# Two small operations a search step, sample digits by block transpose, and a limit for GpSimd on weight rests in a two-layer decoder step

## The chip, the cores and the metric

The kernel runs on one core of one Trainium2 chip. The metric is the device time of one execution in microseconds; the time of a kernel is the median of several runs.

Names of engines in this document: PE is TensorE, DVE is VectorE, ACT is ScalarE, POOL is GpSimd, SP is the engine whose queue starts most transfers.

## The reference, cut to what matters

One inference step of a decoder with two layers, for a prompt of 1024 tokens and 8 sample sequences with 1024 cached tokens each. Layer 0 is forgetting attention beside a gated recurrence, layer 1 is sparse attention, and a feed-forward block follows each. The change lies in layer 1, in the choice of keys:

```python
def dsa_attend(qpos, q, qi, wi, k, v, ki, topk):
    dots = jnp.einsum('bqhd,bkd->bqhk', qi, ki).astype(jnp.float32)
    score = jnp.einsum('bqhk,bqh->bqk', jax.nn.relu(dots), wi.astype(jnp.float32))
    causal = kpos[None, None, :] <= qpos[None, :, None]
    _, idx = lax.top_k(jnp.where(causal, score, -jnp.inf), topk)   # topk = 256
    ...   # attention of q over the chosen keys only
```

Each query has 1024 (prompt, causal) or 1025 (sample) scores and keeps the 256 largest. Everything is float32.

## The kernel before, in words

**How the program is put in order.** Work is written as Python generators ("streams"). Each yields the cost in nanoseconds that its author assumes for what it just emitted, and a driver always resumes the stream with the smallest virtual time. So the order in which instructions are emitted, and with it, mostly, the order of each engine's queue, follows from the yielded numbers; a planner of the framework can still move instructions, and a manual order edge (`late`) ties some matmuls behind the dense products. An engine works its queue strictly in order: an instruction that waits holds up all behind it. A yielded cost is no time on the chip, but it moves where an instruction stands in the queue.

**Layer 1, the stretch that matters.** The main stream multiplies the normed activations by 17 blocks of 128 columns of the projection weights (`dense_cols`). Each block is loaded, rounded by ACT to the hi part (`whif`), the rest (`wlof`) is made by DVE, and PE does 3 products for each of 8 x 3 pieces. Beside it run three kinds of streams:

- `gen_idx` makes the indexer scores of 128 queries (a row block i) against (i + 1) * 128 keys, for i = 2..7 in the groups [2, 3], [4, 5], [6, 7], and starts `top_select` for each group. (Blocks 0 and 1 keep every key.)
- `top_select` finds for every query the 256th largest score, by a search over the 31 bits of the float from the top down: 31 steps, each of which counts how many scores are at or above a candidate. In a step of the kernel before, DVE makes the candidate (`cd = F ^ (1 << b)`); each of the two row blocks is counted, by ACT (a Sign with its sum, `tjk<-sc,small` on ACT) or by DVE (a compare with its sum, L1993); DVE makes `d` from the counts, and then the new `F`: three small DVE operations of 128 x 2 elements. `NACT` says how many of a group's two blocks ACT counts: both of group 2, one of group 4 (640 wide) and one of group 6 (896 wide). DVE counts the other, 768 and 1024 wide; for bits 30 to 16 on a bf16 copy (`top`) that POOL makes. A step yields `early` before the projection is finished and `cost` after. At the end come some whole-row operations that write the mask.
- `gen_dsa_dec` does the same for the 8 samples by hexadecimal digits: 8 steps, in each of which 16 partitions of a sample try 16 candidates. DVE counts (L2263, 1025 wide) and compares with 256; a matmul with a 128 x 128 constant (L2268) adds the comparisons of each 16 partitions, and DVE reads the sum from PSUM. Afterwards the chosen keys' positions are computed (among it the transposes and matmuls at L2324), the keys gathered, and the sample attention done.

When the 17 blocks are done, the attention of layer 1 starts: 8 row blocks by 4 key heads, row block i only once its mask is there. It has scores (`s`, L530), a DVE operation that adds the mask and finds the largest (L533), ACT exponentials, transposes, and products with V (`o`, L2099 up to row block 4 and L2103 from 5). Then come the output projection, and layer 1's feed-forward block.

**POOL** does the rotary products (`raw`, `shf`) and rests (`r1l`) of the projected blocks in this stretch, with operations of 2.4 us each.

The class `Weights` counts the weight blocks that it has split in `self.ns`. The list that it walks through has 21 + 8 blocks for layer 0, 4 for the feed-forward block's last part, 17 + 8 for layer 1, and 4 more: 62, so `ns` runs from 0 to 61, and layer 1's projection has the numbers 33 to 49. Two places ask for an interval of it:

```python
        def phase(n):
            return "" if n < 25 or 93 <= n < 110 else "f"
                    hi, lo = U(..., "whi" + ph), U(..., "wlo" + ph)
                    (gt if self.ns < 3 or 93 <= self.ns < WP else tt)(lo, raw, _r(hi), SUB)
```

`gt` is POOL's operation, `tt` DVE's; a tile's name has an "f" outside the interval.

Of the kernel before, what the change touches and what calls it, by code (L numbers as in the profile page):

```python
# [8 lines left out]
F32 = mybir.dt.float32  # L9
F32R = mybir.dt.float32r  # L10
BF = mybir.dt.bfloat16
# [9 lines left out]
S = 1024  # L21
# [11 lines left out]
def _consts():  # L33
# [31 lines left out]
    c["bm8x128"] = (b8[:, None] == p[None, :] // 16).astype(f)  # L65
    c["grp16"] = ((p[:, None] // 16 == p[None, :] // 16) & (p[:, None] % 16 >= 1)).astype(f)
    c["bd16"] = (p[:, None] // 16 == p[None, :] // 16).astype(f)
# [19 lines left out]
PTAGS.update({k: ("bl", 2) for k in ("ia", "ib", "ka", "kb", "do")})  # L87
WP, DY = 0, 2200.0
NACT = {2: 2, 4: 1, 6: 1}
QID = 0  # L90
# [4 lines left out]
SPARE = {3: (1,), 4: (1,), 5: (1, 3), 6: (1, 3), 7: (1, 3)}  # L95
BFC = True
PLAIN = range(5)
# [62 lines left out]
def build(tc, I, O, C):  # L160
    nc = tc.nc
    with ExitStack() as ctx:
# [68 lines left out]
        def gcopy(out, in_):  # L231
            return (nc.gpsimd if BFC == True else nc.vector).tensor_copy(out=out, in_=in_)

# [1670 lines left out]
        def gen_idx():  # L1904
# [11 lines left out]
            for grp in ([2, 3], [4, 5], [6, 7]):  # L1916
                if grp[0] == 2:
                    s2 = U([128, 1040], F32, "sc")
                    sc[2], sc[3] = s2[:, :384], s2[:, 384:896]
                else:  # L1920
                    for i in grp:
                        sc[i] = U([128, S], F32, "sc")[:, :(i + 1) * 128]
                for i in grp:
                    masks[i] = sc[i].bitcast(BF)[:, :(i + 1) * 128]
                if grp[0] == 2:
                    for t in range(4):
                        yield from need("l1.qi%d" % t)
                        for i in grp:
                            yield from idx_scores(i, 2 * t, 2)
                else:  # L1930
                    for i in grp:
                        yield from idx_scores(i, 0, 8)
                for i in grp:
                    w = sc[i].shape[1]
# [31 lines left out]
        def top_select(grp, rows):  # L1966
# [5 lines left out]

            na = NACT[grp[0]]
            A = slice(0, na)
            F, cd, d = [small("1", [128, 2], nm, bufs=3, dt=I32) for nm in ("tF", "tcd", "td")]
            cnt, thr = small("1", [128, 2], "tcnt", bufs=3), small("1", [128, 2], "tthr", bufs=3)
# [4 lines left out]

            top = {}
            if BFC:
                for j in range(na, 2):
                    n = rows[j][1]
                    top[j] = V([128, 1040], BF, "top")[:, :n]
                    gcopy(top[j], rows[j][0].bitcast(BF).rearrange("p (n e) -> p n e", e=2)[:, :, 1])

            def count(j, th, op, b=0):
                sj, n = rows[j][:2]  # L1990
                if b >= 16 and BFC:
                    sj = top[j]
                nc.vector.tensor_scalar(out=jk[:, 1, :n], in0=sj, scalar1=th, scalar2=None, op0=op, op1=ADD,  # L1993
                                        accum_out=cnt[:, j:j + 1])

            for j in range(2):
                nc.gpsimd.memset(thr[:, j:j + 1], 2 * TOPK - 0.5 - rows[j][1] if j < na else TOPK - 0.5)
            cost, early = CM[grp[0]] * (n1 / 0.96 + 600), CE[grp[0]] * (n1 / 0.96 + 600)
# [5 lines left out]
            ts(F, d, 31, 31, ALU.logical_shift_left, ALU.arith_shift_right)  # L2004
            if na:
                ts(F[:, A], F[:, A], -0x80000000, None, ALU.bitwise_xor)
# [29 lines left out]
            for j, (sj, n, m) in enumerate(rows):  # L2036
                th = thr[:, j:j + 1]
                eq = jk[:, 1]
                ts(eq[:, :n], sj, th, None, ALU.is_equal)
# [109 lines left out]
        def gen_dsa_dec():  # L2149
# [92 lines left out]
            dma(out=dig, in_=C["dig"])  # L2242
            grp = V([128, 128], F32, "grpc")
            dma(out=grp, in_=C["grp16"])
            ti = [small("1", [128, 1], "tdi%d" % x, dt=I32) for x in range(4)]
# [10 lines left out]
            for step in range(8):  # L2256
# [7 lines left out]
                                        op0=ALU.is_ge, op1=ADD, accum_out=cn)  # L2264
                ts(cn, cn, TOPK - 0.5, None, ALU.is_ge)
                yield DY
                p = bank()
                late(mm(p[:, 0:1], lhsT=grp, rhs=cn, start=True, stop=True))  # L2268
                yield 700.0
                sh_ = 28 - 4 * step  # L2270
                if step == 0:
                    ts(sf, p[:, 0:1], 7.5, -16.0, ALU.is_ge, MUL)
                    tt(sf, sf, p[:, 0:1], ADD)
# [358 lines left out]
```

## Time and profile before

| | us |
|---|---|
| median of 3 runs | 2834.91 |
| lowest and highest run | 2833.43, 2839.29 |
| profiled execution | 2833.61 |
| its span, first to last instruction | 2831.9 |

Outside the span lie 1.7 us. In the span PE is busy 90%, DVE 79%, ACT 47% and POOL 47% of the time. Shares over the whole span hide that the stages have different limits, so the rows below are taken from single stretches, in us from the start of the span: 1445 to 1690 (the projection of layer 1 with the searches), 1690 to 1770 and 1770 to 1880 (attention of layer 1 with the searches of groups 4 and 6), and 1880 to 2000 (attention without a search).

### The profile page before, as it was taken

To read this page: it belongs to the slowest core of one execution; us is meant where nothing else is said; L and a number is where in the kernel's file an instruction comes from. 1 tells how busy PE (TensorE), PEld (TensorE's weight loads), DVE (VectorE), ACT (ScalarE), POOL (GpSimd) and SP (SyncE) were. 2 spreads that over 40 slices of the span, in tenths; PEclk is the share of its full clock that TensorE was granted. 3 is DMA by queue.
4 is the path that set the end of the run, shared out by engine and by line. 5 is a ranking of instruction groups with operands and counts; after the bars stand their busy time and mean duration, and the time that the engine had idled before them with its cause. 6 is when DMAs were issued, how large, how long until landed. Compare 5 with 4: busy or idle time off the path is not lost.

```text
span 2831.9 us, 48456 instructions
## 1 busy us (share of the span) xinstructions
PE 2556.9 (90%) x17916; PEld 2391.4 (84%) x17916; DVE 2230.6 (79%) x4125; ACT 1328.7 (47%) x2726; POOL 1337.9 (47%) x992
## 2 busy tenths in 40 slices
PE   7988889989999899999888758999979999899998
PEld 6977788989999899999777744567979999898998
DVE  4466887787777899986468999998477887899995
ACT  4235766344434433433256457779333343533331
POOL 2376454345555666620544525133135555667630
PEclk9999999999999999999989868999989999999999
DMA  4844567304444634322353325321303444644331
GB/s 132 269 149 142 164 213 251 131 16 139 136 154 135 205 126 143 128 98 93 97 154 106 119 77 129 81 59 31 128 23 109 143 147 145 207 135 131 125 105 61
DMA packets 272095, 363.30 MB, mean 128 GB/s; under 512 B 25184, under 2 KB 200456, under 8 KB 271604
## 3 DMA queue, kind: packets, MB, share of 16 engines
q1 hardware_dynamic: 217124, 290.48, 32.1%
q0 software_dynamic: 15120, 49.81, 5.3%
q10 hardware_dynamic: 39616, 19.93, 2.5%
q8 instruction: 141, 2.31, 0.3%
q14 instruction: 94, 0.77, 0.1%
HBM read 252.19 MB, written 108.00 MB: 127 GB/s over the span
## 4 chain that ended last, share of the span: by engine, by line
PE 47%; DVE 21%; issue 4%; ACT 4%; DMA 3%; POOL 2%; SPq 0%; ACTq 0%; DVEq 0%; POOLq 0%
PE d L1501 10%; PE d L1503 9%; PE d L1502 9%; DVE fdu L218 4%; PE d L339 3%; PE d L341 3%; PE d L340 3%; PE s L530 2%; PE o L2099 2%; PE t L251 2%; DVE xT L218 1%; DVE x1a L218 1%; DVE small L229 1%; DVE fd L218 1%; DVE tjk L1993 1%
## 5 line engine op out<-in xcount | busy, mean ns | idle before, releaser
L1501 PE MATMUL d<-xoph,fs 128*128 128x258 f32 x768 | 221.6, 289 | 19.7 <-ACT z L215 13.0
L221 POOL TENSOR_TENSOR fraw<-fraw,small 128x1024 f32<-128x1024 f32 x64 | 134.4, 2104 | 209.9 <-DMA fraw<-in_ffn_w 181.7
L218 DVE TENSOR_TENSOR xT<-xT,d 128x258 f32<-128x258 f32 (+1 forms) x472 | 185.5, 424 | 44.6 <-PE d L341 26.9
L1502 PE MATMUL d<-xoph,fs 128*128 128x258 f32 x768 | 219.2, 286 | 0.0
L1503 PE MATMUL d<-xoph,fs 128*128 128x258 f32 x768 | 218.4, 285 | 0.0
L339 PE MATMUL d<-xh,whif 128*128 128x344 f32 (+1 forms) x616 | 201.9, 329 | 11.4 <-DVE small L226 5.7
L341 PE MATMUL d<-xh,wlof 128*128 128x344 f32 (+1 forms) x616 | 198.0, 325 | 3.9 <-DVE wlof L218 3.9
L340 PE MATMUL d<-xl,whif 128*128 128x344 f32 (+1 forms) x616 | 200.6, 326 | 0.0
L221 POOL TENSOR_TENSOR z<-z 128x516 f32<-128x516 f32 x112 | 168.8, 1507 | 47.0 <-DMA d_zp<-z 39.2
L215 ACT ACTIVATE s<-s,small 128x128 f32<-128x128 f32 (+7 forms) x192 | 149.7, 782 | 66.8 <-DVE small L533 65.5
L339 PE MATMUL d<-xh,whi 128*128 128x344 f32 x504 | 169.9, 338 | 11.4 <-ACT whi L215 5.9
L341 PE MATMUL d<-xh,wlo 128*128 128x344 f32 x504 | 165.0, 330 | 12.2 <-DVE wlo L218 11.8
L1501 PEld LDWEIGHTS d<-xoph,fs 128*128 128x128 f32 x768 | 147.2, 192 | 23.8 <-ACT z L215 16.3
L340 PE MATMUL d<-xl,whi 128*128 128x344 f32 x504 | 167.2, 332 | 0.0
L218 DVE TENSOR_TENSOR fdu<-fraw,fdu 128x256 fp32r<-128x256 f32 x168 | 165.0, 993 | 0.0
L1501 PE MATMUL d<-zoph,fdu 128*128 128x258 f32 x448 | 129.7, 292 | 26.9 <-DVE xT L218 13.7
L1502 PEld LDWEIGHTS d<-xoph,fs 128*128 128x128 f32 x768 | 147.6, 192 | 0.6 <-DVE xoph L218 0.6
L1503 PEld LDWEIGHTS d<-xoph,fs 128*128 128x128 f32 x768 | 147.7, 192 | 0.0
L1503 PE MATMUL d<-xop,fl 128*128 128x258 f32 x512 | 146.3, 286 | 1.4 <-DVE fl L218 1.4
L1501 PE MATMUL d<-xop,fl 128*128 128x258 f32 x512 | 146.4, 286 | 0.0
L1502 PE MATMUL d<-xop,fl 128*128 128x258 f32 x512 | 146.2, 286 | 0.0
L251 PE MATMUL t<-small,s 128*128 128x128 f32 x864 | 139.4, 280 | 5.7 <-DVE tm L218 3.4
(484 smaller groups left out, 9902.2 us busy)
## 6 DMA issues: line engine op xcount, KB each, us to landing
fraw<-in_ffn_w SPq DMA_DIRECT2D x120, 512.0 KB
zr<-d_zp SPq DMA_DIRECT2D x98, 516.0 KB
d_zp<-z POOLq DMA_DIRECT2D x56, 516.0 KB, 3.2
kp<-in_cache_fox_kv SPq DMA_DIRECT2D x64, 256.0 KB
vp<-in_cache_fox_kv SPq DMA_DIRECT2D x64, 256.0 KB
q1b<-d_q ACTq DMA_DIRECT2D x32, 512.0 KB
d_zp<-z SPq DMA_DIRECT2D x28, 516.0 KB
wraw<-in_ab_w_in SPq DMA_DIRECT2D x21, 512.0 KB
```

What stands on the lines that cost most here:

```text
L215: return nc.scalar.activation(out=out, in_=in_, func=func, **kw)
L218: return nc.vector.tensor_tensor(out=out, in0=a, in1=b, op=op)
L221: return nc.gpsimd.tensor_tensor(out=out, in0=a, in1=b, op=op)
L251: return nc.tensor.transpose(out, in_, ident[:n, :n])
L339: mm(ps, lhsT=wh, rhs=ah, start=(j == 0), stop=False)
L340: mm(ps, lhsT=wh, rhs=al, start=False, stop=False)
L341: i = mm(ps, lhsT=wl, rhs=ah, start=False, stop=(j == last))
L530: mm(p[:, :m], lhsT=lh[x], rhs=ks[:, k0:k0 + m], start=(x == 0), stop=(x == 1 and not dg))
L1501: mm(o, lhsT=wh[:, k], rhs=hi[:, cols], start=(start and k == 0), stop=False, skip_group_check=not start)
L1502: mm(o, lhsT=wh[:, k], rhs=lo[:, cols], start=False, stop=False, skip_group_check=not start)
L1503: i = mm(o, lhsT=wl[:, k], rhs=hi[:, cols], start=False, stop=(k == nk - 1), skip_group_check=not start)
L2099: mm(po[:64], lhsT=VF[g // 2][:, kb, 64 * (g % 2):64 * (g % 2) + 64], rhs=ph, start=(kb == 0), stop=(kb == i))
```

## The change

- **Search step.** `F` now carries the next candidate itself, so that a step has two small operations behind the counts instead of one ahead and two behind: `e` is (count below the bound) * 2^b, and `F = (F ^ 2^(b-1)) ^ e`. `SGP` is False, so its branch for POOL is not built.
- **Who counts.** `ONA = (2, 4)`: ACT counts both blocks of groups 2 and 4, all at the width of the wider block (512 and 768), with the narrower block's last 128 columns filled with `LOW`; DVE counts both of group 6 (896 and 1024). The bf16 copies `top` (2 POOL copies, 2 buffers of the V pool) are gone.
- **Sample digits.** The matmul L2268 of each of the 8 steps is gone. DVE writes the comparison into 32 columns, transposes 32 x 32 blocks, multiplies by a constant of 128 x 32 and sums over 32 columns. The virtual cost of 700 for the matmul goes (8 times), and two later yields grow, from 26000 to 32000 and from 4000 to 10000.
- **Weight rests.** `WP` goes from 0 to 110 in the condition above.

```diff
-WP, DY = 0, 2200.0
-NACT = {2: 2, 4: 1, 6: 1}
+WP, DY = 110, 2200.0
+ONA, SGP = (2, 4), False
...
-                    sc[2], sc[3] = s2[:, :384], s2[:, 384:896]
+                    sc[2], sc[3] = s2[:, :512], s2[:, 512:1024]
...
+                if grp[0] in ONA:
+                    nc.gpsimd.memset(sc[grp[0]][:, (grp[0] + 1) * 128:], LOW)
...
-            na = NACT[grp[0]]
+            na = 2 if grp[0] in ONA else 0
...
-                    top[j] = V([128, 1040], BF, "top")[:, :n]
-                    gcopy(top[j], rows[j][0].bitcast(BF).rearrange("p (n e) -> p n e", e=2)[:, :, 1])
...
+            ts(F, F, (1 << 30) - (0x80000000 if na else 0), None, ALU.bitwise_xor)
             yield cost
             for b in range(30, -1, -1):
-                ts(cd, F, 1 << b, None, ALU.bitwise_xor)
                 for j in range(2):
-                    if j < na:
-                        act(jk[:, 0, :rows[j][1]], rows[j][0], AF.Sign, bias=cd[:, j:j + 1].bitcast(F32),
+                    if na:
+                        act(jk[:, 0, :n1], rows[j][0], AF.Sign, bias=F[:, j:j + 1].bitcast(F32),
                             accum_out=cnt[:, j:j + 1])
                     else:
-                        count(j, cd[:, j:j + 1].bitcast(F32), ALU.is_ge, b)
-                stt(d, cnt, 1.0, thr, MUL, ALU.is_ge)
-                stt(F, d, b, F, ALU.logical_shift_left, ALU.bitwise_xor)
+                        count(j, F[:, j:j + 1].bitcast(F32), ALU.is_ge)
...
+                    ts(e, cnt, least, float(1 << b), ALU.is_lt, MUL)
+                    stt(F, e, (1 << b) >> 1, F, ALU.bitwise_xor, ALU.bitwise_xor)
                 yield cost if "l1.in" in flags else early
...
-                ts(cn, cn, TOPK - 0.5, None, ALU.is_ge)
+                ts(c32, cn.to_broadcast([128, 32]), TOPK - 0.5, None, ALU.is_ge)
+                nc.vector.transpose(t32, c32)
+                tt(t32, t32, g32, MUL)
+                nc.vector.tensor_reduce(out=cn, in_=t32, axis=AX.X, op=ADD)
                 yield DY
-                p = bank()
-                late(mm(p[:, 0:1], lhsT=grp, rhs=cn, start=True, stop=True))
-                yield 700.0
...
-                    ts(sh, p[:, 0:1], float(1 << sh_), None, MUL)
+                    ts(sh, cn, float(1 << sh_), None, MUL)
...
-            yield 26000
+            yield 32000
...
-            yield 4000
+            yield 10000
```

## Rows read from the trace of the kernel before

**Rows 1.** Busy time of each engine in four stretches: PE, PEld, DVE, ACT, POOL, PE clock.
```profile
1445.00:1690.00 245.00, 177.67 (x986) 166.85 (x986) 222.51 (x459) 140.63 (x332) 113.44 (x64) 0.84 0.37 110
1690.00:1770.00 80.00, 64.26 (x247) 35.70 (x246) 71.33 (x252) 60.30 (x164) 35.92 (x38) 0.81 0.53 132
1770.00:1880.00 110.00, 106.76 (x498) 59.70 (x497) 102.00 (x293) 79.20 (x181) 18.95 (x17) 1.00 0.28 74
1880.00:2000.00 120.00, 114.92 (x667) 92.98 (x666) 98.28 (x258) 110.84 (x231) 48.95 (x56) 1.00 0.16 47
```

**Rows 2.** Waits, 1445 to 1690: waiter, what ended it, us, times, longest.
```profile
ACT tjk L215 <- DVE small L226: 56.9, 20, 7.0
...
PEld b L2268 <- DVE small L226: 18.0, 4, 6.2
PE b L2268 <- DVE small L226: 16.7, 4, 6.0
...
PE b L2324 <- DVE small L229: 13.6, 1, 13.6
DVE small L229 <- ACT tjk L215: 11.6, 10, 2.2
```

**Rows 3.** DVE by line and shape, 1445 to 1690: busy us, mean ns | idle before.
```profile
L226 DVE TENSOR_SCALAR small<-small 128x2 int32<-128x2 int32 x65 | 25.6, 395 | 0.9
L229 DVE SCALAR_TENSOR_TENSOR small<-small 128x2 int32<-128x2 int32 x55 | 22.7, 414 | 0.5
...
L1993 DVE TENSOR_SCALAR_CACHE_REDUCE tjk<-top,small 128x768 bf16<-128x768 bf16 x15 | 15.1, 1004 | 0.1
...
L1993 DVE TENSOR_SCALAR_CACHE_REDUCE tjk<-sc,small 128x768 bf16<-128x768 f32 x4 | 4.0, 1012 | 0.1
```

**Rows 4.** DVE in order of time, near 1610: start us, us, operation.
```profile
1609.39 2.25 DVE L226 TENSOR_SCALAR small<-small 128x2 int32<-128x2 int32 x1
...
1612.76 2.28 DVE L229 SCALAR_TENSOR_TENSOR small<-small 128x2 int32<-128x2 f32 x1
```

**Rows 5.** POOL in order of time, the same moments.
```profile
1609.20 2.42 POOL L221 TENSOR_TENSOR raw<-raw,ropc 128x1032 f32<-128x1032 f32 x1 [1.35 <-DVE small L229]
1611.58 3.44 POOL L221 TENSOR_TENSOR shf<-shf,rops 128x1032 f32<-128x1032 f32 x1
```

**Rows 6.** The search's tile over the span: durations min/median/max, first and last start.
```profile
L1993 DVE TENSOR_SCALAR_CACHE_REDUCE tjk<-top,small x30: 995/1132/1279, 1503.6 to 1769.1; 128x768 bf16<-128x768 bf16 x15, 128x1024 bf16<-128x1024 bf16 x15
```

**Rows 7.** DVE by line and shape, 1650 to 1670.
```profile
L2333 DVE TENSOR_REDUCE tmpd<-tmpd 128x16 f32<-128x128 f32 x1 | 0.4, 363 | 0.0
...
L226 DVE TENSOR_SCALAR small<-small 128x2 f32<-128x2 f32 x2 | 0.3, 158 | 0.0
```

**Rows 8.** DVE by line and shape, 1690 to 1770.
```profile
L1993 DVE TENSOR_SCALAR_CACHE_REDUCE tjk<-sc,small 128x768 bf16<-128x768 f32 x14 | 14.1, 1010 | 0.2
...
L226 DVE TENSOR_SCALAR small<-small 128x2 int32<-128x2 int32 x23 | 3.8, 179 | 0.3
```

**Rows 9.** DVE by line and shape, 1770 to 1880.
```profile
L226 DVE TENSOR_SCALAR small<-small 128x2 int32<-128x2 int32 x19 | 3.5, 186 | 0.3
...
L1993 DVE TENSOR_SCALAR_CACHE_REDUCE tjk<-sc,small 128x896 bf16<-128x896 f32 x2 | 2.3, 1144 | 0.0
```

**Rows 10.** ACT by line and shape, 1770 to 1880.
```profile
L215 ACT ACTIVATE tjk<-sc,small 128x896 bf16<-128x896 f32 x16 | 16.6, 1035 | 5.6 <-DVE small L226 5.5
...
L215 ACT ACTIVATE s<-s,small 128x768 f32<-128x768 f32 x7 | 6.5, 934 | 6.2 <-DVE small L533 6.1
L215 ACT ACTIVATION_READ_ACCUMULATOR tjk<-sc,small 128x1 f32 x16 | 3.1, 191 | 0.0
```

**Rows 11.** ACT by line and shape, 1445 to 1690.
```profile
L215 ACT ACTIVATE tjk<-sc,small 128x640 bf16<-128x640 f32 x19 | 15.7, 828 | 30.6 <-DVE small L226 23.7 <-DVE small L229 6.8
...
L215 ACT ACTIVATE tjk<-sc,small 128x896 bf16<-128x896 f32 x6 | 6.2, 1040 | 0.2
```

**Rows 12.** The tile wlof, 1300 to 1700: durations min/median/max, first and last start.
```profile
L218 DVE TENSOR_TENSOR wlof<-wrawf,whif x16: 1211/1226/2506, 1322.9 to 1663.9; 128x1024 fp32r<-128x1024 f32 x16
```

More of the change, by code (lines that the diff above doesn't have):

```diff
@@ L65, in _consts @@
     c["bm8x128"] = (b8[:, None] == p[None, :] // 16).astype(f)
-    c["grp16"] = ((p[:, None] // 16 == p[None, :] // 16) & (p[:, None] % 16 >= 1)).astype(f)
+    f32 = np.arange(32)
+    c["grp32"] = ((p[:, None] % 32 // 16 == f32[None, :] // 16) & (f32[None, :] % 16 >= 1)).astype(f)
     c["bd16"] = (p[:, None] // 16 == p[None, :] // 16).astype(f)
@@ L95 @@
 SPARE = {3: (1,), 4: (1,), 5: (1, 3), 6: (1, 3), 7: (1, 3)}
-BFC = True
 PLAIN = range(5)
@@ L231, in gcopy @@
         def gcopy(out, in_):
-            return (nc.gpsimd if BFC == True else nc.vector).tensor_copy(out=out, in_=in_)
+            return nc.gpsimd.tensor_copy(out=out, in_=in_)
         def bcast(src):
@@ L1918, in gen_idx @@
                     s2 = U([128, 1040], F32, "sc")
-                    sc[2], sc[3] = s2[:, :384], s2[:, 384:896]
+                    sc[2], sc[3] = s2[:, :512], s2[:, 512:1024]
                 else:
                     for i in grp:
-                        sc[i] = U([128, S], F32, "sc")[:, :(i + 1) * 128]
+                        sc[i] = U([128, S], F32, "sc")[:, :(grp[1] + 1) * 128 if grp[0] in ONA else (i + 1) * 128]
                 for i in grp:
@@ L1932, in gen_idx @@
                         yield from idx_scores(i, 0, 8)
+                if grp[0] in ONA:
+                    nc.gpsimd.memset(sc[grp[0]][:, (grp[0] + 1) * 128:], LOW)
                 for i in grp:
-                    w = sc[i].shape[1]
+                    w = (i + 1) * 128
                     nc.gpsimd.affine_select(out=sc[i][:, w - 128:w], in_=sc[i][:, w - 128:w], pattern=[[-1, 128]],
@@ L1966, in top_select @@
         def top_select(grp, rows):
-            na = NACT[grp[0]]
+            na = 2 if grp[0] in ONA else 0
             A = slice(0, na)
-            F, cd, d = [small("1", [128, 2], nm, bufs=3, dt=I32) for nm in ("tF", "tcd", "td")]
+            F, d, e = [small("1", [128, 2], nm, bufs=3, dt=I32) for nm in ("tF", "td", "tcd")]
             cnt, thr = small("1", [128, 2], "tcnt", bufs=3), small("1", [128, 2], "tthr", bufs=3)
@@ L1980, in top_select, with count @@
             nc.gpsimd.memset(cu[:, 0:1], 0.0)
[L1982 to L1985, printed above, removed]
-                    top[j] = V([128, 1040], BF, "top")[:, :n]
-                    gcopy(top[j], rows[j][0].bitcast(BF).rearrange("p (n e) -> p n e", e=2)[:, :, 1])
-            def count(j, th, op, b=0):
+            def count(j, th, op):
                 sj, n = rows[j][:2]
-                if b >= 16 and BFC:
-                    sj = top[j]
-                nc.vector.tensor_scalar(out=jk[:, 1, :n], in0=sj, scalar1=th, scalar2=None, op0=op, op1=ADD,
+                nc.vector.tensor_scalar(out=jk[:, 1, :n], in0=sj[:, :n], scalar1=th, scalar2=None, op0=op, op1=ADD,
                                         accum_out=cnt[:, j:j + 1])
-            for j in range(2):
-                nc.gpsimd.memset(thr[:, j:j + 1], 2 * TOPK - 0.5 - rows[j][1] if j < na else TOPK - 0.5)
+            least = 2 * TOPK - 0.5 - n1 if na else TOPK - 0.5
             cost, early = CM[grp[0]] * (n1 / 0.96 + 600), CE[grp[0]] * (n1 / 0.96 + 600)
@@ L2004, in top_select @@
             ts(F, d, 31, 31, ALU.logical_shift_left, ALU.arith_shift_right)
-            if na:
-                ts(F[:, A], F[:, A], -0x80000000, None, ALU.bitwise_xor)
+            ts(F, F, (1 << 30) - (0x80000000 if na else 0), None, ALU.bitwise_xor)
             yield cost
             for b in range(30, -1, -1):
-                ts(cd, F, 1 << b, None, ALU.bitwise_xor)
                 for j in range(2):
-                    if j < na:
-                        act(jk[:, 0, :rows[j][1]], rows[j][0], AF.Sign, bias=cd[:, j:j + 1].bitcast(F32),
+                    if na:
+                        act(jk[:, 0, :n1], rows[j][0], AF.Sign, bias=F[:, j:j + 1].bitcast(F32),
                             accum_out=cnt[:, j:j + 1])
                     else:
-                        count(j, cd[:, j:j + 1].bitcast(F32), ALU.is_ge, b)
-                stt(d, cnt, 1.0, thr, MUL, ALU.is_ge)
-                stt(F, d, b, F, ALU.logical_shift_left, ALU.bitwise_xor)
+                        count(j, F[:, j:j + 1].bitcast(F32), ALU.is_ge)
+                if na and SGP:
+                    nc.gpsimd.tensor_scalar(out=d, in0=F, scalar1=(1 << b) >> 1, scalar2=None, op0=ALU.bitwise_xor)
+                    nc.gpsimd.tensor_scalar(out=e, in0=cnt, scalar1=least, scalar2=float(1 << b), op0=ALU.is_lt, op1=MUL)
+                    gt(F, d, e, ALU.bitwise_xor)
+                else:
+                    ts(e, cnt, least, float(1 << b), ALU.is_lt, MUL)
+                    stt(F, e, (1 << b) >> 1, F, ALU.bitwise_xor, ALU.bitwise_xor)
                 yield cost if "l1.in" in flags else early
@@ L2038, in top_select @@
                 eq = jk[:, 1]
+                sj = sj[:, :n]
                 ts(eq[:, :n], sj, th, None, ALU.is_equal)
@@ L2242, in gen_dsa_dec @@
             dma(out=dig, in_=C["dig"])
-            grp = V([128, 128], F32, "grpc")
-            dma(out=grp, in_=C["grp16"])
+            grp = V([128, 3, 32], F32, "grpc")
+            dma(out=grp[:, 0], in_=C["grp32"])
+            g32, c32, t32 = [grp[:, x] for x in range(3)]
             ti = [small("1", [128, 1], "tdi%d" % x, dt=I32) for x in range(4)]
```

4 lines of the change are left out of this document (2 added, 2 removed).

## Prediction, written before the changed kernel was run

> **What bounds the kernel now.** I went from the page's shares to the chain of waits, saw that the searches lie in it between 1445 and 1880 us, and then took the busy time of the engines by stretch [rows 1]. Three stretches differ.
>
> In stretch A (1445 to 1690, projection and searches) DVE is busy 222.5 of 245 us, PE only 177.7, at a mean granted clock of 0.84, ACT 140.6. So DVE sets the pace there. The waits of A say the same from the other side [rows 2]: ACT waits 56.9 us for a DVE operation of 128 x 2 elements ahead of its Sign, PE waits 18.0 + 16.7 = 34.7 us for DVE's comparison ahead of the digit matmul, and 13.6 us at L2324. DVE itself waits for another engine mainly in one place: 11.6 us for ACT's Sign.
>
> In stretch B (1690 to 1770, attention begins) DVE is busy 71.3 of 80 us and PE 64.3. In stretch C (1770 to 1880) PE is busy 106.8 of 110 us at full clock and DVE 102.0: both are nearly full, and DVE has 8.0 us left. From 1880 on no search runs.
>
> What makes DVE slow in A is to be seen in the small operations. The same form takes 395 ns on average in A [rows 3] and 179 and 186 ns in B and C [rows 8, 9]. The difference is POOL: an operation of 2 elements took 2.25 us while POOL's rotary product of 2.42 us ran, and the next one 2.28 us beside a product of 3.44 us [rows 4, 5]. The counts don't suffer from it: 995 to 1279 ns over both widths, smallest to largest [rows 6].
>
> **The change part by part.** The search has 93 steps; 55 lie in A, by the number of the second of the two operations behind the counts [rows 3], and the other 38 in B and C.
>
> *One small operation fewer a step.* A: 55 operations. At the unhindered 0.18 us [rows 8, 9] that is 9.9 us; at A's own mean of 0.395 us [rows 3] 21.7 us. The waits behind POOL in it, 55 x 0.215 = 11.8 us, may only move to the next operation, so I take 14 us. The lower bound is 8.7 us, by a small DVE operation that waited for nothing, 0.158 us [rows 7]. B: 23 x 0.179 = 4.1 us; C: 19 x 0.186 = 3.5 us.
>
> *Candidates ready a step early.* ACT's Sign waited for `cd`, made at the start of its own step. The new `F` is made at the end of the step before, one yield earlier in the queues. So ACT can count long before DVE comes to `e`, and DVE's 11.6 us of waiting for ACT should nearly go. Against it: group 4's step now needs two Signs 768 wide, near 2 x (0.934 + 0.191) = 2.25 us [rows 10], where one of 0.828 us ran beside DVE's own count [rows 11]. Not hidden at all, 19 such steps would cost 43 us; but a step of group 4 came only about every 10 us (19 from 1503.6 us [rows 6] to the end of A). I take 7 us saved, from 11 saved to 5 lost. ACT's load rises by 19 x (2.25 - 1.02) = 23 us and falls by 6 counts of 896, 6 x 1.23 = 7 us [rows 11]: some 157 of 245 us, still with room.
>
> *Group 4's counts leave DVE.* A: 15 at 1.004 and 4 at 1.012 us = 19.1 us [rows 3]. POOL is busy 113.4 of 245 us, 46%; counts that ran beside POOL, without being hindered, hid that much of its time, and what follows them may wait instead: at least 19.1 x 0.54 = 10 us. I take 14. B: 12 of the 14 at 1.010 us, less one more count at the end, which now checks both blocks: 11.1 us [rows 8].
>
> *Group 6's counts of 896 come to DVE,* at 1.144 us each [rows 9]. Their number is ACT's before: of 31, 6 in A [rows 11], 16 in C [rows 10], so 9 in B: 6.9, 10.3 and 18.3 us more. One count at the end falls away in C (1.1 us). That DVE now counts in f32 where it read a bf16 copy costs nothing: 768 wide took 1.004 and 1.012 us [rows 3].
>
> *Sample digits.* Eight times a comparison over 32 columns, a transpose, a product and a sum in place of one comparison. Neither the transpose nor the 32-wide forms are in the trace. Small DVE operations take 0.158 us, a sum over 128 columns 0.363 us [rows 7]: with three more at 0.16 to 0.36 us, 8 x 3 x 0.25 = 6 us, from 4 to 9, and 12 if two of them also wait behind POOL as in rows 3. On PE the 34.7 us of waiting go; they are no gain of their own as long as DVE sets the pace, since PE would wait for DVE's weight rests next. The later yields move the samples' transposes and L2324 behind more dense work; what is late there is PE's 13.6 us, the same cover. The samples' result is needed only by the output projection, behind all of the prompt's attention, so the shift has room.
>
> *Weight rests: nothing.* Both WP = 0 and WP = 110 leave the condition false, for the list has 62 blocks and `ns` never reaches 93. The trace shows it too: layer 1's rests are the tile `wlof`, with the "f" that the same interval takes away, and DVE makes them, to 1663.9 us [rows 12]. No row of POOL takes them over.
>
> *Also at nothing:* the fill with `LOW` and the copies `top` (POOL, which has half of A free), and the two V buffers set free, which could at most help B's waits (PE idles 15.7 us there).
>
> **The sum.** A: -14 - 7 - 14 + 6.9 + 6 = -22 us, which shorten A, as DVE sets its end. B: DVE -4.1 - 11.1 + 10.3 = -4.9 us; PE has gaps that DVE only partly makes, so -3. C: DVE +18.3 - 3.5 - 1.1 = +13.7 us against 8.0 us left: between +5.7, if every gap can be used, and +13.7. I take +8. Together -17 us against the profiled execution's 2833.6 us: 2817. That execution is 1.3 us below the median of the runs shown, so the two are the same for this purpose.
>
> **The rivals.**
>
> *The waits behind POOL move on (no change).* What a small operation waited was POOL's time, not its own, and fewer unhindered counts leave fewer places to hide it. Then A gives -9 (bare time) - 10 + 6.9 + 9 - 4 = -7 us, B -1, C +8: 2834. For it: the removed counts are just what is never hindered. Against it: POOL is idle more than half of A, and the wait for ACT is real idle time. Chance 0.15. The Trainium skill, "SBUF — State Buffer", section "Who interferes with whom", states this rule: VectorE and GpSimd share a port pair that one instruction holds whole and the other waits for; VectorE needs it with two SBUF inputs or in a mode that reads through both ports, and not for a compare that writes out its sum or for a reduction. Rows 4 to 6 agree, as far as they go.
>
> *Group 6 on DVE becomes the bound (slower).* In C each step puts 1.14 + 1.28 us of counts in front of attention's mask operations, with PE full. If none of DVE's gaps can be used, C grows by 13.7 us, and by 18.3 if the removed small operations return nothing either. It decides where A and B together give less than that, which is so if A ends by PE's own order rather than DVE's. With A and B at 0: 2833.6 + 14 = 2848. For it: 102 of 110 us. Against it: A's 91% against PE's 73%. Chance 0.16.
>
> *PE runs free (faster still).* Without the digit matmuls PE loses none of the 34.7 us, its clock of 0.84 in A rises, and nothing but DVE's load counts: 222.5 - 14 - 14 + 6.9 + 6 = 207 us, so A shrinks by up to 38; with B at -5 and C at +6, 2797. Chance 0.15.
>
> *The third part acts after all.* 9 rests of A would leave DVE, 9 x 1.23 = 11 us, for POOL, and the time would be near 2806. The tile's name speaks against it. Chance 0.02.
>
> **How the numbers follow.** The forecast (2806 to 2828) has 0.52, the rivals 0.15, 0.16, 0.15 and 0.02. A measurement of this kernel can tell about 0.2% from no change, 5.7 us. Faster: forecast, free PE and third part, with 0.02 of the first rival: 0.71. Same: 0.13. Slower: 0.16. The range of 2795 to 2838 takes in A's bounds (-38 to about -7) with C's (+6 to +14), and leaves out the upper half of the slow rival and little below.
>
> **What the profile after would show.** Two small operations for each step on DVE, and ACT's waits for DVE in the projection far below 56.9 us. No L2268 on PE, and PE's waits for DVE gone there or moved to `wlof`. The attention begins near 1668 us instead of 1690. DVE without gaps from then to the last mask, with pairs of 896 and 1024 counts, and PE below its 97%. `wlof` still on DVE, 17 of them. I am wrong if the attention begins when it did before (A was not DVE's), if DVE's small operations average far over 0.4 us (the waits moved), or if the last stretch with a search grows by over 14 us.

## The result and the profile after

The changed kernel is slower: 2864.45 us median (2855.92 to 2870.88, five runs) beside 2836.6 us for the kernel before (2833.43 to 2844.57, five runs), a ratio of 1.0092 with a 95% interval of 1.0068 to 1.0115. The forecast was 17 us faster. The profiled execution has a span of 2862.7 us, 30.8 us more than before's 2831.9.

First the busy time by stretch of the changed kernel, the view of [rows 1].

```profile
1445.00:1690.00 245.00, 195.48 (x1059) 179.17 (x1058) 202.60 (x383) 155.64 (x370) 120.03 (x69) 0.85 0.42 122
1690.00:1770.00 80.00, 66.11 (x276) 36.70 (x275) 71.74 (x228) 62.07 (x159) 37.22 (x41) 0.85 0.54 127
1770.00:1880.00 110.00, 101.39 (x449) 55.89 (x448) 92.69 (x266) 68.40 (x161) 10.19 (x13) 0.97 0.22 59
1880.00:2000.00 120.00, 85.92 (x467) 68.63 (x466) 107.49 (x264) 79.68 (x167) 35.41 (x41) 0.87 0.11 32
```

In stretch A DVE has 20 us less work and PE gets 18 us more done: A looks as forecast. DVE also has less in C. The loss lies where no search was to run any more: from 1880 to 2000 PE falls from 114.92 to 85.92 us of 120, while DVE rises from 98.28 to 107.49.

Next the attention's first scores, its last products and the mask scans of the searches: tiles q1b, o and tcu, with durations and the first and last start.

```profile
L530 PE MATMUL s<-ks,q1b x384: 222/396/797, 1670.9 to 2018.1; 128*128 128x512 f32 x96, 128*128 128x128 f32 x32, 128*128 128x256 f32 x32, 128*128 128x384 f32 x32
...
L2100 PE MATMUL o<-ph,vs x168: 388/398/776, 1870.8 to 2031.6; 128*128 128x512 f32 x168
...
L2037 DVE TENSOR_TENSOR_SCAN tcu<-tjk x6: 931/1624/2281, 1699.1 to 1931.5; 128x384 f32<-128x384 bf16 x1, 128x512 f32<-128x512 bf16 x1, 128x640 f32<-128x640 bf16 x1, 128x768 f32<-128x768 bf16 x1
```

The same three lines of the kernel before:

```profile
L530 PE MATMUL s<-ks,q1b x384: 222/393/745, 1686.5 to 1985.5; 128*128 128x512 f32 x96, 128*128 128x128 f32 x32, 128*128 128x256 f32 x32, 128*128 128x384 f32 x32
...
L2103 PE MATMUL o<-ph,vs x168: 387/397/505, 1873.5 to 1997.1; 128*128 128x512 f32 x168
...
L2040 DVE TENSOR_TENSOR_SCAN tcu<-tjk x6: 958/1619/2259, 1666.9 to 1870.0; 128x384 f32<-128x384 bf16 x1, 128x512 f32<-128x512 bf16 x1, 128x640 f32<-128x640 bf16 x1, 128x768 f32<-128x768 bf16 x1
```

So the attention begins 15.6 us earlier, its last mask (block 7) is scanned 61.5 us later, and it ends 34.5 us later. What comes behind it is as long as before (831 us against 835).

Two stretches of 20 us show what the end of the wait looks like, and a row of the waits from 1880 to 1960 names it.

```profile
1900.00:1920.00 20.00, 4.05 (x25) 2.87 (x23) 19.15 (x46) 5.42 (x13) 4.38 (x5) 0.70 0.08 23
1920.00:1940.00 20.00, 9.49 (x41) 7.80 (x42) 19.65 (x37) 4.64 (x9) 0.00 (x0) 0.62 0.09 27
```

```profile
PE o L2100 <- DVE small L533: 27.8, 2, 25.8
```

PE does 13.5 us of work in 40 us at a granted clock of 0.70 and 0.62, and DVE is full: blocks 0 to 5 are used up, and all wait for the last steps of group 6's search. The order on DVE says the same: block 6's scan stands behind 128 of the attention's 192 mask operations (L533), which are all those of blocks 0 to 5; before, it stood behind 98.

The busy time of the search's own instructions (tile tjk; DVE and ACT) shows when they ran, in the changed kernel and then in the kernel before.

```profile
1740.00:1760.00 20.00, 9.05 (x15) 6.13 (x12) 0.91 0.48 110
1760.00:1780.00 20.00, 0.65 (x2) 7.14 (x14) 1.00 0.42 99
1780.00:1800.00 20.00, 0.00 (x0) 6.12 (x12) 1.00 0.27 73
1800.00:1820.00 20.00, 10.36 (x17) 1.01 (x2) 0.89 0.13 34
```

```profile
1740.00:1760.00 20.00, 6.09 (x13) 4.11 (x8) 1.00 0.43 113
1760.00:1780.00 20.00, 11.45 (x14) 1.13 (x2) 0.91 0.63 151
1780.00:1800.00 20.00, 6.03 (x9) 5.55 (x10) 1.00 0.27 67
1800.00:1820.00 20.00, 5.54 (x10) 4.59 (x10) 1.00 0.29 70
```

In the changed kernel DVE counts next to nothing for 40 us (0.65 us), while ACT is still at group 4. In DVE's order of time these are group 6's 1024 wide counts of bit 17, of bit 16 and the closing one, before and then after:

```profile
1743.82 1.28 DVE L1993 TENSOR_SCALAR_CACHE_REDUCE tjk<-top,small 128x1024 bf16<-128x1024 bf16 x1
...
1769.09 1.28 DVE L1993 TENSOR_SCALAR_CACHE_REDUCE tjk<-top,small 128x1024 bf16<-128x1024 bf16 x1
...
1849.69 1.28 DVE L1993 TENSOR_SCALAR_CACHE_REDUCE tjk<-sc,small 128x1024 bf16<-128x1024 f32 x1
```

```profile
1759.36 1.28 DVE L1987 TENSOR_SCALAR_CACHE_REDUCE tjk<-sc,small 128x1024 bf16<-128x1024 f32 x1
...
1818.30 1.28 DVE L1987 TENSOR_SCALAR_CACHE_REDUCE tjk<-sc,small 128x1024 bf16<-128x1024 f32 x1
...
1921.38 1.28 DVE L1987 TENSOR_SCALAR_CACHE_REDUCE tjk<-sc,small 128x1024 bf16<-128x1024 f32 x1
```

Of the 71.7 us by which the closing one is later, 15.5 came before the pause, 33.7 are a longer pause, and 22.5 are longer steps (17 from the one count to the next, 4.7 us each before, 6.1 after).

### The profile page after: what moved, and what is told of

It is laid out like the page before. It is cut to its first block, busy times and chain, and to the rows that moved or that the text cites. A ratio compares the mean times of both kernels' runs of the same rounds, so it can differ in the third digit from the quotient of the medians.

```text
span 2862.7 us, 48320 instructions
## 1 busy us (share of the span) xinstructions
PE 2562.5 (90%) x17900; PEld 2390.6 (84%) x17900; DVE 2239.4 (78%) x4055; ACT 1327.8 (46%) x2726; POOL 1336.0 (47%) x986
## 4 chain that ended last, share of the span: by engine, by line
PE 46%; DVE 20%; issue 5%; ACT 4%; DMA 3%; POOL 2%; SPq 0%; ACTq 0%; DVEq 0%; POOLq 0%
PE d L1501 10%; PE d L1503 10%; PE d L1502 10%; DVE fdu L218 4%; PE d L341 3%; PE d L339 3%; PE d L340 3%; PE s L530 2%; PE o L2096 2%; PE t L251 2%; DVE xT L218 1%; DVE small L226 1%; PE o L2100 1%; DVE tjk L1987 1%; DVE x1a L218 1%
## 5 line engine op out<-in xcount | busy, mean ns | idle before, releaser
L251 PEld LDWEIGHTS t<-small,s 128*128 128x128 f32 x864 | 104.7, 145 | 51.2 <-issue 14.0
L1503 PE MATMUL d<-xop,fl 128*128 128x258 f32 x512 | 146.1, 286 | 1.4 <-DVE fl L218 1.4
L1501 PE MATMUL d<-xop,fl 128*128 128x258 f32 x512 | 146.1, 285 | 0.0
```

The lines of the kernel that those rows point to most:

```text
L251: return nc.tensor.transpose(out, in_, ident[:n, :n])
L1501: mm(o, lhsT=wh[:, k], rhs=hi[:, cols], start=(start and k == 0), stop=False, skip_group_check=not start)
L1503: i = mm(o, lhsT=wl[:, k], rhs=hi[:, cols], start=False, stop=(k == nk - 1), skip_group_check=not start)
```

## The experiments

Three theories came from this. *Theory 1:* the pause is an order of the program. DVE's counts of all groups and the closing mask operations write to one row of the tile `tjk`, so group 6's step of bit 16, written behind group 4's masks, stands behind them in DVE's queue; group 4 ends 50 us later (block 4's scan at 1811.1 against 1760.9), and group 6 with it. *Theory 2:* the 896 wide counts now on DVE make group 6's late steps longer (the rival "group 6 on DVE becomes the bound"). *Theory 3:* sample digits and later yields moved the queues.

The median of before was 2843.8, 2837.7, 2844.9 and 2838.9 us beside the four groups of runs, so the ratios are to be read, not the microseconds; where a theory forecast microseconds, I compare them as ratios to the 2836.6 us of the result. Times of the profiled executions also differ by up to 7 us ahead of the changed part.

**Buffers of their own.** `own_row` for group 6, `own_row_g4` for group 4.

```
+ cj = V([128, 1040], BF, "tjk6") if grp[0] == 6 else jk[:, 1]
- out=jk[:, 1, :n]   ...   eq = jk[:, 1]
+ out=cj[:, :n]      ...   eq = cj
```

> The changed kernel, but group 6's counts and closing mask operations write to a buffer of their own and not to the row of tjk that groups 2 and 4 and the sample digits write too. Every operation and its load stay. Theory 1 (order through the shared row: in program order group 6's steps from bit 16 on stand behind group 4's closing operations, which end 50 us later than before): group 6's search no longer pauses between 1760 and 1815 us, its masks come before the prompt attention's blocks 6 and 7 need them, PE's gaps of 1880 to 1960 us go, and with the projection's 16 us kept the time is 2805 to 2825 us. Theory 2 (the 896 wide counts make DVE the bound): DVE does the same work, so 2855 to 2870 us. Theory 3 (the later yields and the sample digits moved the queues): no change either, 2855 to 2870 us.

> The changed kernel, but it is group 4 whose counts and closing mask operations have a buffer of their own; group 6 shares the old row with group 2 and the sample digits only. In the queue of DVE group 6's last step then stands ahead of block 6 of the attention and no longer behind all of block 5, while group 4's masks stand as late as in the changed kernel. Theory 1: group 6's pause goes, but blocks 4 and 5 still wait for group 4's masks near 1820 us, so only a part comes back: 2825 to 2845 us. Theories 2 and 3: 2855 to 2870 us.

Measured: own_row 1.0053 (1.0036 to 1.0071), own_row_g4 1.0020 (1.0002 to 1.0038). The pause of 1760 to 1815 us goes in both, so the row does make it. But without it group 6 runs far ahead in own_row: 25 of its 31 steps lie ahead of the attention, which begins at 1713.1 us. This is own_row's busy time from 1640 to 1700 us, and its longest wait of PE there:

```profile
1640.00:1700.00 60.00, 7.63 (x39) 6.97 (x39) 59.73 (x172) 29.94 (x68) 6.69 (x5) 0.57 0.00 0
```

```profile
PE b L251 <- DVE hk L218: 40.1, 1, 40.1
```

DVE is full and PE does 7.63 us of work. So the row also holds the search back where it would be in the way. own_row_g4 lies in theory 1's range (0.996 to 1.003) and gives back most of the loss with every operation left in place; its last scan comes at 1898.2 us, not 1931.5. So DVE's load alone doesn't make the loss: what counts is where the late steps stand in the order and when the last one ends. own_row lies in no theory's range.

**Parts of the change.** `digits_alone` puts the digits and yields into the kernel before, `search_alone` takes them out of the changed one.

> The kernel before with only the sample digits by transpose and the two later yields; the search as it was. Theory 1 (the search's change made the loss): group 4 keeps its one Sign and its end near 1757 us, so the time is near that of before, 2825 to 2840 us. Theory 3: here is the loss, 2850 to 2865 us. In the queue of DVE group 6's last step stands behind more of the attention's mask operations than before (424 of them against 372), which speaks for a part of the loss here.

> The changed search, with the sample digits by matmul and the old yields. Theory 1: group 4's two Signs keep its end late and group 6 behind it, 2845 to 2865 us. Theory 2: as much, 2845 to 2865 us, with DVE busy throughout from 1770 us on and no pause of group 6. Theory 3: the gain of the search without the loss, 2810 to 2825 us.

Measured: digits_alone 0.9987 (0.9973 to 1.0001), search_alone 1.0041 (1.0026 to 1.0056). Theory 3 falls as a cause alone, but the two parts together (1.0092) cost more than their sum (1.0028). digits_alone changes the digits and the later yields at once, so which of the two moves the search's steps isn't separated.

**Who counts what, in the kernel before**, with its three small operations and old digits.

```
- NACT = {2: 2, 4: 1, 6: 1}
+ NACT = {2: 2, 4: 2, 6: 0}     # split_2_0;  4: 2, 6: 1 is split_2_1;  4: 1, 6: 0 is split_1_0
```

> The kernel before, with three small operations a step and its old digits, but with the changed kernel's split of the counts: both blocks of group 4 by ACT, both of group 6 by DVE. Theory 1 (two Signs a step make group 4 end late, and group 6 resumes only behind group 4's masks): group 4's first mask some 20 to 30 us behind 1761 us, group 6's last count near 1900 us, and 1.003 to 1.010 of before. Theory 2 (DVE's load by the 896 wide counts alone): the same time, but group 6 without a pause. Were the loss in the two small operations or the digits, it would be 0.998 to 1.002.

> As split_2_0, but block 6 is still counted by ACT and only block 7 by DVE: group 4's part of the split alone. Theory 1: most of the loss is here, 1.003 to 1.008 of before, with group 4's first mask 20 to 30 us later. Theory 2: no 896 wide count on DVE, so no loss, 0.997 to 1.001.

> As split_2_0, but group 4 is split as before (one block each) and both blocks of group 6 are counted by DVE: group 6's part of the split alone. Theory 1: group 4's masks come near 1761 us as before, group 6 resumes there and 17 steps of some 6.4 in place of 4.6 us end some 25 us later than before's 1856 us, which the attention's blocks 6 and 7 can just bear: 1.000 to 1.004. Theory 2: the whole loss, 1.004 to 1.010.

Measured: 1.0078 (1.0060 to 1.0096), 0.9994 (0.9980 to 1.0008) and 1.0102 (1.0082 to 1.0123). On the question of where the loss sits theory 2 is right: with group 4's two Signs alone (split_2_1) block 4's scan is as late as 1793.4 us and nothing is lost; with group 6 on DVE alone (split_1_0) the whole loss is there. In split_2_0 group 6 pauses for 72 us, as theory 1 had said; split_1_0 shows that the loss doesn't need that pause. Its mask scans in split_1_0, and DVE by line and shape there from 1770 to 1930 us:

```profile
L2040 DVE TENSOR_TENSOR_SCAN tcu<-tjk x6: 957/1625/2279, 1674.8 to 1929.5; 128x384 f32<-128x384 bf16 x1, 128x512 f32<-128x512 bf16 x1, 128x640 f32<-128x640 bf16 x1, 128x768 f32<-128x768 bf16 x1
```

```profile
L1993 DVE TENSOR_SCALAR_CACHE_REDUCE tjk<-sc,small 128x1024 bf16<-128x1024 f32 x17 | 21.6, 1270 | 0.1
L1993 DVE TENSOR_SCALAR_CACHE_REDUCE tjk<-sc,small 128x896 bf16<-128x896 f32 x17 | 19.4, 1142 | 0.3
```

Group 6 pauses here no longer than before (25.5 us against 25.3), yet its last 17 steps come 7.6 us apart, not 4.7. The second count costs 1.14 us, the step grows by 2.8. The rest is the attention's work between the counts: among these 17 steps stand 81 of its mask operations (L533) in DVE's queue, among the same 17 before 46. DVE is busy 121.9 us of the 128 from 1790 to 1918. Whether another order, with less of the attention among these steps, would take the loss away was not tried.

**Group 6's counts off DVE.** `g6_on_act`: ACT counts all groups (`ONA = (2, 4, 6)`, a row of its own for group 6's Signs).

> The changed kernel, but group 6 too is counted by ACT, both blocks 1024 wide, with a row of its own for what the Signs write. DVE loses 62 counts of 1.14 to 1.28 us, 75 us. Theory 2: the loss goes, and with the projection's gain the time is 0.988 to 0.995 of before. Theory 1: group 6 runs past group 4, its masks come by 1850 us, and what stays is the attention's wait for group 4's masks near 1810 us, as in own_row_g4: 0.996 to 1.003.

Measured: 1.0079 (1.0062 to 1.0097), a miss for both theories as I had put them. ACT counts group 6 beside group 4 in one queue, and group 4 is what suffers: block 5's scan at 1860.7 us. The waits from 1770 to 1880:

```profile
PE o L2096 <- ACT ph L215: 34.3, 1, 34.3
```

The kernel moves the counts and gives them a row at once, so which of the two lets group 6 run ahead of group 4 isn't separated.

**Group 6's split undone in the changed kernel**, alone, with the old digits, and with a buffer of its own for group 4.

```
- na = 2 if grp[0] in ONA else 0
+ na = 2 if grp[0] in ONA else 1
+ elif na == 1:
+     stt(d, cnt, 1.0, thr, MUL, ALU.is_lt)
+     stt(F, d, b, F, ALU.logical_shift_left, ALU.bitwise_xor)
+     ts(F, F, (1 << b) >> 1, None, ALU.bitwise_xor)
```

> The changed kernel with one thing undone: group 6 has block 6 counted by ACT and block 7 by DVE again, and for that three small operations a step. Groups 2 and 4, the digits and the yields stay changed. Theory 2 (the 896 wide counts on DVE make each late step of group 6 longer, 6.1 to 7.5 us in place of 4.8, and the last mask comes too late for blocks 6 and 7): the last mask near 1900 us in place of 1932, and with the projection's gain 0.988 to 0.998 of before. Theory 1 (group 4's late end and the shared row): group 4 ends as late as in the changed kernel and still holds group 6, so 1.004 to 1.009.

> As g6_split_back, with the sample digits by matmul and the old yields too: two small operations in groups 2 and 4 and group 4's two Signs are all that is left of the change. If the digits only hid nothing, it lies with g6_split_back within 0.2%. If the digits' part makes group 4 later and that still counts, it is faster than g6_split_back by 0.3% or more, 0.985 to 0.995. If the projection's gain came from the digits, it is slower, near 1.000.

> As g6_split_back, and group 4's counts and closing operations on DVE write to a buffer of their own, so that group 6 needn't stand behind them. If the hold through the shared row still costs something once group 6 is split again, it is faster than g6_split_back by 0.3% or more. If the hold only shifts work within the slack that the attention leaves, the two agree within 0.2%.

Measured: 1.0004 (0.9988 to 1.0019), 1.0017 (1.0003 to 1.0032), 1.0056 (1.0039 to 1.0073). The loss goes with the split, as theory 2 says, but no gain is left: 1.0004 lies between the ranges of the two theories, with the last scan at 1914.5 us, not 1900. The old digits change nothing that can be told (within 0.2% of it); the buffer does harm here, against both forecasts, and why is open. Of the third kernel only the times are used.

**What the late steps cost.** `g6_half_search` leaves out group 6's steps below bit 16, `g4_g6_half_search` group 4's too.

```
- for b in range(30, -1, -1):
+ for b in range(30, 15 if grp[0] == 6 else -1, -1):      # the second: grp[0] >= 4
```

> The changed kernel, but group 6's search stops after bit 16: its last 16 steps are left out, so its masks come from a coarse threshold. Everything else is as in the changed kernel, group 4's late end too. If the loss is the attention's wait for the last masks, it goes: the last mask comes by 1870 us, and the time is 0.984 to 0.994 of before. If the attention itself had become slower (its own work on DVE, the clock, waits for group 4), a loss stays: 0.998 or more.

> The changed kernel, with both group 4's and group 6's search stopped after bit 16, so that the masks of blocks 4 to 7 come from coarse thresholds; the rest as changed. In the runs so far the attention's last product comes at the latest of three times: 310 us behind its first score, 172 us behind block 5's mask, 98 us behind block 7's mask. g6_half_search ended by the second. With group 4 early too only the first is left: 10 to 15 us below g6_half_search, 0.988 to 0.991 of before. If the three limits are only a fit and the attention is slow for another reason, it lies with g6_half_search, 0.993 to 0.996.

Measured: 0.9943 (0.9929 to 0.9956) and 0.9910 (0.9891 to 0.9930). PE from 1880 to 1960 us in g6_half_search, and the attention's last products in g4_g6_half_search:

```profile
1880.00:1960.00 80.00, 79.36 (x462) 65.00 (x462) 69.36 (x188) 77.53 (x162) 35.09 (x40) 1.00 0.16 47
```

```profile
L2100 PE MATMUL o<-ph,vs x168: 388/397/505, 1855.0 to 1978.3; 128*128 128x512 f32 x168
```

PE is full again. The runs take away the late steps' work on DVE together with their lateness and don't separate the two. With the last masks early, the changed kernel lies 0.57% below before, or 16 us: the 17 that I had forecast, but with work left out to pay for it.

**The groups exchanged.** ACT counts groups 2 and 6, DVE group 4 (`ONA = (2, 6)`); the second kernel gives group 6's Signs a row of their own.

> The changed kernel with the two groups exchanged: ACT counts both blocks of groups 2 and 6 (group 6 1024 wide), DVE both of group 4. Two small operations a step everywhere. DVE counts 31 x (640 + 768) columns in place of 31 x (896 + 1024). By the three limits: group 4 ends some 30 us earlier than in the changed kernel, group 6's late steps no longer stand in DVE's queue as counts, the last mask comes 20 to 40 us earlier, and the time is 0.992 to 1.000 of before. If what costs is that a group has no count on ACT or that DVE has no count of group 6 to fill its gaps, it stays at 1.005 or more.

> As g6_act_g4_dve, and group 6's Signs write to a buffer of their own, so that they needn't stand behind group 2's in program order. In g6_on_act that let group 6 run ahead of group 4 on ACT; here group 4 is on DVE and has nothing to lose by it. If the shared row holds group 6 back, its last mask comes earlier and the time is 0.990 to 0.998 of before; if group 6 is set by its own chain of two Signs and two small operations, it lies with g6_act_g4_dve within 0.2%.

Measured: 1.0020 (1.0010 to 1.0030) and 0.9984 (0.9973 to 0.9994). The second is faster than the changed kernel and lies 0.16% below the one before, less than the 0.2% that I count as a change. The first lies in neither of its two ranges; the second is 0.36% faster than the first, so group 2's row did hold group 6 back. Its mask scans:

```profile
L2037 DVE TENSOR_TENSOR_SCAN tcu<-tjk x6: 958/1834/2936, 1670.1 to 1883.3; 128x384 f32<-128x384 bf16 x1, 128x512 f32<-128x512 bf16 x1, 128x640 f32<-128x640 bf16 x1, 128x768 f32<-128x768 bf16 x1
```

Block 7's scan is 48 us earlier than in the changed kernel.

## Why the prediction was wrong

The profiled executions of 16 kernels together show one pattern. "Steps" are those of the 93 search steps that had been counted when the first score began, from the counts and Signs in order of time (the two half searches have 77 and 61 in all); times in us.

```
kernel                    ratio   first score  steps  scan 5   scan 7   last product
before                    1       1686.5       55     1771.1   1870.0   1997.1
after                     1.0092  1670.9       43.5   1821.6   1931.5   2031.6
own_row                   1.0053  1713.1       75.5   1818.9   1764.9   2024.5
own_row_g4                1.0020  1668.3       43.5   1843.2   1898.2   2023.2
digits_alone              0.9987  1675.5       46.5   1796.1   1905.4   2003.2
search_alone              1.0041  1685.1       55.5   1802.3   1923.8   2023.8
split_2_0                 1.0078  1680.8       51.5   1799.1   1923.1   2018.7
split_2_1                 0.9994  1673.7       52     1804.0   1903.7   1999.6
split_1_0                 1.0102  1696.5       54     1792.0   1929.5   2028.7
g6_on_act                 1.0079  1673.8       46     1860.7   1890.4   2033.3
g6_split_back             1.0004  1664.9       43.5   1816.6   1914.5   2010.4
g6_split_back_old_digits  1.0017  1676.1       51.5   1802.5   1909.6   2008.8
g6_half_search            0.9943  1666.4       43.5   1820.5   1847.7   1989.8
g4_g6_half_search         0.9910  1669.0       43.5   1733.1   1817.1   1978.3
g6_act_g4_dve             1.0020  1678.7       46.5   1796.5   1899.3   2009.2
g6_act_own_row_g4_dve     0.9984  1679.5       52     1778.4   1883.3   1997.4
```

The last product comes at the latest of three times: 310 us behind the first score, 172 us behind block 5's scan, 98 us behind block 7's. That fits 13 of the 16 within 3 us; own_row_g4, g6_act_g4_dve and g6_act_own_row_g4_dve end 8 to 12 us later than it gives. It is a fit to these runs with three constants, made before the last three of them: the first bears it out (1979 against 1978.3), the other two are among those that miss it. Before, the first limit sets the end (1996.5), and block 7's mask has 28 us to spare (1870.0 + 98 = 1968). After, the third sets it: 1931.5 + 98 = 2029.5.

By the prediction's own steps:

*The steps that failed* are the two that give B and C: "55 lie in A ... and the other 38 in B and C", and C priced by DVE's load against the 8.0 us left. The sum let the time from the first score to the last product grow by 5 us (B -3, C +8); it grew by 50.1. Each step shows by itself. search_alone has 55.5 search steps done at its first score, as many as before, and group 6 on DVE beside the rest of the search's change: there the time is 28.1 us longer (21.6 in split_1_0, with group 6's split alone). digits_alone keeps group 6's split and has only 46.5 steps done: 17.1 us longer.

A did end earlier, by 15.6 us, or by 22 counted from the first count of group 2, which came 6.7 us later in this execution. My -22 looks exact, and is so by luck: 11.5 steps of the search had not been done by then. They moved behind the first score, and there each is paid in front of the attention's own work. With as many steps done as before, search_alone begins its attention only 1.4 us earlier, or 8 us counted in the same way, where my terms for the search's change alone add up to -28. The kernels with about 52 steps done begin at 1674 to 1681 us, those with 43.5 at 1665 to 1671.

*Group 6 in C, "I take +8".* Price and place of the rival were right in kind (each step puts both counts in front of the mask operations), its size was not: I took 14 to 18 us of DVE's load, as if the stretch only grew by what DVE lacks. In C DVE became less busy, 92.7 us in place of 102.0, as the last 8 of group 6's steps moved out of C behind 1880 us. What counts is when the chain of steps ends: the last scan came 61.5 us later, which is its slack of 28 us and 33 more. I gave this rival 0.16 and said that it needs A and B to give less than it costs; I took them at nothing for its 2848. The loss came although A ended about as early as I had forecast.

*"One small operation fewer", -14.* It gave about 5. DVE by line and shape after, 1445 to 1690 us, the view of [rows 3]:

```profile
L226 DVE TENSOR_SCALAR small<-small 128x2 int32<-128x2 f32 x50 | 28.3, 567 | 15.9 <-ACT tjk L215 15.8
L229 DVE SCALAR_TENSOR_TENSOR small<-small 128x2 int32<-128x2 int32 x46 | 23.8, 518 | 0.5
L218 DVE TENSOR_TENSOR small<-small 128x1 int32<-128x1 int32 x30 | 18.8, 628 | 0.8
...
L226 DVE TENSOR_SCALAR small<-small 128x1 int32<-128x1 int32 x30 | 4.5, 151 | 0.6
```

The third small operation of a step before, in the same view of that kernel:

```profile
L229 DVE SCALAR_TENSOR_TENSOR small<-small 128x2 int32<-128x2 f32 x55 | 20.6, 376 | 12.1 <-ACT tjk L215 11.6
```

A step has two small operations of 567 + 518 = 1085 ns in place of three of 395 + 414 + 376 = 1185 ns. So 0.10 us a step, not 0.25: the waits behind POOL moved on, as the first rival said, and the operations average over the 0.4 us that I had named. The trace shows the waits one by one. Of all DVE operations on 128 x 2 in A, 26 of 183 took over 0.4 us before and 22 of 107 after, and each of these ended within 0.04 us of the end of a POOL operation. What they took beyond 0.16 us each adds up to 42.5 us before and 40.8 after. Two of them after, from DVE's and POOL's order of time:

```profile
1633.70 2.39 DVE L226 TENSOR_SCALAR small<-small 128x2 int32<-128x2 f32 x1
1636.12 2.35 DVE L229 SCALAR_TENSOR_TENSOR small<-small 128x2 int32<-128x2 int32 x1
```

```profile
1632.76 3.30 POOL L221 TENSOR_TENSOR raw<-raw,ropc 128x1032 f32<-128x1032 f32 x1 [2.74 <-DVE shf L1767]
1636.03 2.43 POOL L221 TENSOR_TENSOR shf<-shf,rops 128x1032 f32<-128x1032 f32 x1
```

*"Candidates ready a step early", -7.* ACT's waits for a step's small operations did fall, to 39.1 + 9.5 = 48.6 us in the two rows below. Before, they were 75.2 us: the prediction's 56.9 leaves out a second row of the same view, the 18.3 us here.

```profile
ACT tjk L215 <- DVE small L229: 18.3, 4, 7.5
```

But the saving was to be DVE's wait for ACT, which was nearly to go, and that rose from 11.6 to 15.8. Waits of the changed kernel, 1445 to 1690 us, as in [rows 2]:

```profile
ACT tjk L215 <- DVE small L229: 39.1, 14, 8.1
...
PEld d L341 <- DVE wlof L218: 18.5, 3, 7.9
PE d L341 <- DVE wlof L218: 17.5, 3, 7.6
...
DVE small L226 <- ACT tjk L215: 15.8, 9, 3.4
...
ACT tjk L215 <- DVE small L226: 9.5, 4, 6.1
```

*Sample digits, +6.* Right in size. The tile grpc gives the four operations of a digit:

```profile
L226 DVE TENSOR_SCALAR grpc<-small x8: 156/173/181, 1510.9 to 1591.7; 128x32 f32<-128x32 f32 x8
L2265 DVE STREAM_TRANSPOSE grpc<-grpc x8: 190/210/213, 1514.5 to 1592.9; 128x32 f32<-128x32 f32 x8
L218 DVE TENSOR_TENSOR grpc<-grpc x8: 177/192/2059, 1520.2 to 1594.1; 128x32 f32<-128x32 f32 x8
L2267 DVE TENSOR_REDUCE small<-grpc x8: 170/186/189, 1520.5 to 1597.5; 128x1 f32<-128x32 f32 x8
```

PE's wait behind the digits became one behind `wlof`, as I had said. Its 34.7 us were misread, though: the two rows are the same four waits, seen once at the weight load (PEld, 18.0 us) and once at the product behind it (PE, 16.7 us), so PE lost 16.7 us there, and in the same way loses 17.5 now. The rival in which PE runs free had half as much to free as it names. And "no gain of their own" was wrong in effect: in digits_alone the attention begins with only 46.5 steps done. That shift costs nothing alone (0.9987), and together with group 6 on DVE the ratio is 1.0092 with it and 1.0041 without.

*Weight rests, nothing.* Right: `wlof` is still made by DVE.

Of my falsifiers two came true: the small operations average 0.57 and 0.52 us, over the 0.4 that I had named, and the stretch from the first score to the last product grew from 310.6 to 360.7 us. Why group 4 ends later in every kernel with a part of the change and its whole search is not settled: block 4's scan comes 24 us later with the digits alone, 32 with the two Signs, 21 with group 6 on DVE, 50 with all of the change, and 9 at the least, in the best kernel.

## What to carry to other kernels

Ask of a search or any other chain beside dense work by when its last result is needed and how much slack it has; a stretch that gets shorter may only have handed the chain's steps on to the next one, so count the steps done at its end. Where an engine is full, a 1.14 us operation added to each step of a chain can cost more than twice that, if more of the other work then comes to stand between two steps in its queue: count what stands there. An operation that is taken away gives back its own time, and what it waited for may wait in the next one. A scratch row that several streams share is a part of the order: giving one its own can free it or let it run ahead of what matters more.

## What the runs showed of the hardware

In stretch A of the changed kernel a single-input operation on 128 x 1 took 151 ns on average, the same line on 128 x 2 567 ns, and a two-input one on 128 x 1 628 ns (the rows above). Seven of the 30 single-input ones on 128 x 1 began while a POOL operation ran, and none of these took over 160 ns; the ones on 128 x 2 that took over 0.4 us ended with POOL's operation. Transposes and sums of 32 columns never took over 213 ns, the product of two such inputs once 2059. The Trainium skill, "SBUF — State Buffer", section "Who interferes with whom", has VectorE and GpSimd contend for the ports that they share when VectorE reads two inputs from SBUF or runs in a mode that uses both ports; the two-input rows and the reductions agree, and no run here tells whether it is such a mode that delays 2 elements and not 1.
